# Eight rotary transfers queued behind the next chunk's softmax scaling on GpSimd

## The chip, the cores and the metric

The kernel runs on one core of one Trainium2 chip. The metric is the device time of one execution in microseconds, the median of several runs. The core's engines work side by side, each through its own queue in order: TensorE (PE, matmuls and transposes; its weight loads are listed as PEld), VectorE (DVE), ScalarE (ACT), GpSimd (POOL) and SyncE (SP, which here only issues DMA transfers).

## The reference, cut to what matters

One encoder block over 16 learned meta tokens and 1024 input tokens, width 1024. A combined projection feeds a retention branch (4 heads) and a windowed softmax attention (8 heads in 2 groups, head size 128); both are gated, projected, merged, projected again, normalised and added to the input. The change lies in the attention and its rotary positions:

```python
def _rotary(t, pos):
    ...
    t1, t2 = tf[..., :half], tf[..., half:]
    return jnp.concatenate([t1 * cos - t2 * sin, t2 * cos + t1 * sin], axis=-1)

# attention: each block of 128 queries sees its own and the two neighbouring blocks
# of keys within +-128, 16 meta keys, and a learned sink logit per head
m = jnp.maximum(jnp.max(s, axis=-1, keepdims=True), sink_l)
p = jnp.exp(s - m)
p = p / (jnp.sum(p, axis=-1, keepdims=True) + jnp.exp(sink_l - m))
```

## The kernel before

The program is written in a tile language: the source gives the work and its priority, a scheduler with a model of the engines' times fixes each engine's order, and semaphores are placed by dependence. `tc.issue_after(i)` (and `follow`, which stacks several of them) adds the rule that what is issued inside stands behind instruction `i` in the queue of the same engine. TensorE's order in the attention stage is thus written out by hand: almost everything follows `latest`, the last matmul so far.

All matmuls are done in three products of a high and a low half (`mm3`, lines 76 to 78), so that each operand is first split: a rounded high half on ScalarE (or GpSimd, `pool_hi`, line 89) and the remainder on VectorE (`dve_lo`, line 92).

**The attention's chunks.** There are 32 chunks: four pairs of heads `hp`, each with eight blocks `n` of 128 queries; chunk 8 hp + n. Iteration k of the loop in `attention` does four things in this order on TensorE:

- `stage1` of chunk k + 1: the scores (`ps`), then on VectorE the mask and row minimum (`nm`, line 1423), on ScalarE the exponentials (line 1426), on VectorE the reciprocal of the sum (`den`, line 1430), on GpSimd the scaling of both sides by `den` (line 1439) and two small copies of the meta columns (`pm2`, line 89).
- `stage2` of chunk k: transposes of the scaled weights (`pt`, lines 1455 to 1460), then their split into `pah`/`pal`, `pbh`/`pbl` and `pm`.
- `fill`: a number of projection steps for later chunks, from a list of generators. `FILL` gives the number per chunk: 9, 9, 7, 7, 7, 7, 6, 6 for the first head pair, 7 each for the second, 7, 6, 6, 6, 6, 6, 6, 5 for the third, then 5.
- `stage3` of chunk k - 1: the weights times the values (`po`).

So a chunk's scaling has one `fill` and one `stage3` in which to be done before TensorE needs it.

**The projection steps.** The steps of all `fill`s are numbered through. A block of queries (`aq{hp}_{i}{e}`: head pair, half of the tokens, head of the pair; 512 columns) or of keys (`ak{g}_{i}`: group, quarter of the tokens) takes eight steps, one for each slice of the inputs. At the end of the eighth, `rope_late` turns the block: VectorE multiplies it by sine into `m` and by cosine into `o` (lines 184, 185), and GpSimd issues two transfers (line 187) that add the two halves of `m`, swapped, onto `o`. Key blocks are 256 or 272 columns wide, each transfer of one 64 partitions. GpSimd's queue works in order, so an issue waits there for VectorE's products, and what is behind it waits too.

**The hooks.** The table `BEGUN` says which other work is issued at which step: among it `split_q(hp, e, i)`, which splits a turned block of queries into `aqh`/`aql` (lines 669 and 92), and `keys(g, i)`, which splits a turned block of keys into `kTh`/`kTl` (lines 715 and 92). Both wait for the landing of that block's two transfers. With `FILL` above, step 23 lies in the `fill` of chunk 2, 31 in chunk 3, 47 in chunk 6, 71 in chunk 9, 79 in chunk 11, 119 in chunk 16, 127 in chunk 18 and 151 in chunk 22. Steps 90 and 91 both lie in chunk 12, 136 and 138 in chunk 19, 126 in chunk 17.

Of the kernel before, what the change touches and what calls it, by code (L numbers as in the profile page):

```python
# [10 lines left out]
ALU = mybir.AluOpType  # L11
# [28 lines left out]
def block_kernel(ctx: ExitStack, tc: tile.TileContext, x0, xT, x, meta, w_in, w_rb, w_ab, w_out, post_w,  # L40
                 rope, tab, out):
    nc = tc.nc
# [31 lines left out]
    def mm3(o, ah, al, bh, bl, first, last, free_group=False):  # L74
        kw = {"skip_group_check": True} if free_group else {}
        nc.tensor.matmul(o, ah, bh, start=first, stop=False, **kw)  # L76
        nc.tensor.matmul(o, al, bh, start=False, stop=False, **kw)  # L77
        latest[:] = [nc.tensor.matmul(o, ah, bl, start=False, stop=last, **kw).ins]  # L78
        return latest[0]
# [8 lines left out]
    def pool_hi(o, i):  # L88
        return nc.gpsimd.tensor_scalar(o, i, 1.0, 1.0, op0=ALU.mult, op1=ALU.mult).ins  # L89
# [87 lines left out]
    cr = ra.tile([P, T], F32, name="cr")  # L177
    sr = ra.tile([P, T], F32, name="sr")

    def rope_late(t, a, b, o, nm):  # L180

        n = b - a
        m = ra.tile([P, 512], F32, tag="m", bufs=4, name=f"m_{nm}")
        nc.vector.tensor_tensor(m[:, 0:n], t[:, 0:n], sr[:, a:b], ALU.mult)
        nc.vector.tensor_tensor(o[:, 0:n], t[:, 0:n], cr[:, a:b], ALU.mult)
        for r in (0, 64):
            nc.gpsimd.dma_start(o[64 - r:128 - r, 0:n], m[r:r + 64, 0:n], accum_op=ALU.add)

    def rope_evac(t, a, b, o, nm):
        n = b - a  # L190
# [250 lines left out]
    def gen_qk(h):  # L441
        w = load_w(w_in, U_QK + h)
        q, kt = [], ra.tile([P, 4, 272], F32, tag="kp", bufs=2, name=f"kr{h}")
        qk[h] = (q, kt)
        for i, (a, b) in enumerate(PIECES):
            t = yield from proj(w, P, a, b, f"pk{h}_{i}")
            rope_late(t, a, b, kt[:, i], f"k{h}_{i}")
            yield
        for i, (a, b) in enumerate(HALVES):
            t = yield from proj(w, 0, a, b, f"pq{h}_{i}")  # L450
            o = ra.tile([P, 512], F32, tag="q", bufs=6, name=f"qr{h}_{i}")
            rope_late(t, a, b, o, f"q{h}_{i}")
            q.append(o)
            yield
# [206 lines left out]
    def split_q(hp, e_, i):  # L661

        o = aq[hp][e_, i].rearrange("p (t q) -> p t q", q=64)
        if (hp, i) not in aqs:
            aqs[hp, i] = [aw.tile([P, 1024], R, tag=f"aq{t}", bufs=2, name=f"aq{t}{hp}_{i}") for t in "hl"], set()
            if len(aqs) == 1:
                aw.tile([P, 48], F32, name="space_aq")
        h, l = (t.rearrange("p (t e q) -> p t e q", e=2, q=64)[:, :, e_] for t in aqs[hp, i][0])
        nc.scalar.copy(h, o)
        dve_lo(l, o, h)  # L670
        aqs[hp, i][1].add(e_)
# [18 lines left out]
    def gen_aq(hp, i, es=(0, 1)):  # L690
        if not i:
            if hp not in wq:
                wq[hp] = load_w(w_in, U_AQ + hp)
            aq[hp] = {}
        a, b = HALVES[i]
        for e_ in es:
            t = yield from proj(wq[hp], P * e_, a, b, f"paq{hp}_{i}{e_}")
            o = ra.tile([P, 512], F32, tag="q", bufs=6, name=f"aq{hp}_{i}{e_}")
            rope_late(t, a, b, o, f"aq{hp}_{i}{e_}")
            aq[hp][e_, i] = o  # L700
            yield
# [158 lines left out]
    softmax, last = [], {}  # L860
# [525 lines left out]
    def attention():  # L1386
# [4 lines left out]
        def window(n, x_):  # L1391

            if n == 0:
                return 0, 272, (late_mask if x_ else mask[0][:, 144:416]), [(0, 0), (1, 128)], 256
            start = 272 * ((n - 1) // 2) + 128 * ((n - 1) % 2) + 64 * x_
            wid = (208 if x_ else 272) if n == 7 else 336
            own, moff = (128, 256) if n % 2 else (144, 128)
            blocks = [(n - 1, -64 * x_), (n, own - 64 * x_), (n + 1, 272 - 64 * x_)]
            return start, wid, mask[0][:, 0:wid], blocks[:2 if n == 7 else 3], moff - 64 * x_

        def stage1(hp, n):
            g = hp // 2
            kh, kl = (t.rearrange("p a b -> p (a b)") for t in kT[g])
            i = n // 4
            nm_ = ap.tile([P, 2], F32, tag="nm", bufs=3, name=f"nm{hp}_{n}")
            den = ap.tile([P, 2], F32, tag="den", bufs=3, name=f"den{hp}_{n}")
            pp = weights[n % 2]
            sides = []
            for e_ in range(2):
                if (hp, i) not in aqs or e_ not in aqs[hp, i][1]:  # L1410
                    split_q(hp, e_, i)
            for x_ in range(2):
                start, wid, seen, blocks, moff = window(n, x_)
                a_, b_ = (t[:, P * (2 * (n % 4) + x_):P * (2 * (n % 4) + x_ + 1)] for t in aqs[hp, i][0])
                s = p2(f"ps{hp}_{n}_{x_}")
                mm3(s[:, 0:wid], a_, b_, kh[:, start:start + wid], kl[:, start:start + wid], True, True)
                if n == 0 and hp:
                    raw[x_] = aw.tile([P, 337], F32, tag=f"raw{x_}", bufs=1, name=f"raw{hp}_{x_}")
                r = raw[x_]
                for c in ({0: (272, 336), 7: (208,)} if x_ else {0: (0,)}).get(n, ()):  # L1420
                    nc.vector.tensor_copy(r[:, c:c + 1], nsink[:, hp:hp + 1])
                o, w0 = (0, 64) if x_ else (1, 1)
                nc.vector.tensor_tensor_reduce(r[:, o:o + wid], s[:, 0:wid], seen, -SCALE,  # L1423
                                               nsink[:, hp:hp + 1], ALU.add, ALU.min, nm_[:, x_:x_ + 1])

                last["exp"] = nc.scalar.activation(pp[:, x_, w0 - o:w0 - o + 1 + wid], r[:, 0:1 + wid], AF.Exp,  # L1426
                                                   scale=-1.0, bias=nm_[:, x_:x_ + 1],
                                                   accum_out=den[:, x_:x_ + 1]).ins
                sides.append((wid, w0, blocks, moff))
            last["sum"] = nc.vector.reciprocal(den, den).ins  # L1430
            softmax.append(last["sum"])
            both = ap.tile([P, 2, 2, NM], F32, tag="pm2", bufs=2, name=f"pm2_{hp}_{n}")
            ends = hp == 3 and n > 5
            for x_, (wid, w0, _, _) in enumerate(sides):
                v = pp[:, x_, w0:w0 + wid]
                if ends:
                    softmax.append(nc.scalar.activation(v, v, AF.Copy, scale=den[:, x_:x_ + 1]).ins)
                else:
                    nc.gpsimd.tensor_scalar(v, v, den[:, x_:x_ + 1], 1.0, op0=ALU.mult, op1=ALU.mult)  # L1439
            for x_, (_, w0, _, moff) in enumerate(sides):  # L1440
                w_ = pp[:, x_, w0 + moff:w0 + moff + NM].unsqueeze(1).to_broadcast([P, 2, NM])
                if ends:
                    softmax.append(nc.scalar.copy(both[:, x_], w_).ins)
                else:
                    pool_hi(both[:, x_], w_)
            pt = [lambda o, x_=x_, w0=w0: pp[:, x_, w0 + o:w0 + o + P] for x_, (_, w0, _, _) in enumerate(sides)]
            st1[hp, n] = (pt, [b for _, _, b, _ in sides], both.rearrange("p a b c -> p (a b c)"))

# [62 lines left out]
        with follow(*latest):  # L1511
            stage1(0, 0)
        for k, (hp, n) in enumerate(chunks):
            ends = k >= len(chunks) - 2
# [4 lines left out]
            if k + 1 < len(chunks):  # L1519
                with follow(*latest, *marks("oa", "lo")):  # L1520
                    stage1(*chunks[k + 1])
                if chunks[k + 1] == (1, NB - 1):
                    keys(1, 0)
# [18 lines left out]
            if k in (12, 14, 21):  # L1542
# [11 lines left out]
             61: [(sum_row, 2, 0)], 62: [(sum_row, 2, 1)], 65: [(sum_fetch, 3)], 66: [(split_q, 1, 0, 1)],  # L1554
             68: [(half_w, 'k', 1, 0)], 72: [(half_w, 'k', 1, 1)], 73: [(split_q, 1, 1, 1)], 75: [(sum_row, 3, 0)],
             76: [(sum_row, 3, 1)], 79: [(sum_fetch, 4)], 82: [(split_q, 2, 0, 0)], 88: [(sum_row, 4, 0)],
             89: [(sum_row, 4, 1)], 90: [(split_q, 2, 1, 0)], 92: [(sum_fetch, 5)], 100: [(sum_row, 5, 0)],
             101: [(sum_row, 5, 1)], 102: [(fetch_aq, 3)], 104: [(keys, 1, 1)], 105: [(sum_fetch, 6)],
             110: [(split_q, 2, 0, 1)], 116: [(keys, 1, 2)], 117: [(half_w, 'q', 3, 0)], 121: [(half_w, 'q', 3, 1)],
             122: [(pre_fetch, 9)], 123: [(sum_row, 6, 0)], 124: [(sum_row, 6, 1)], 126: [(split_q, 2, 1, 1)],  # L1560
             127: [(sum_fetch, 7)], 133: [(pre_sum, 9, 0)], 134: [(pre_sum, 9, 1)], 136: [(keys, 1, 3)],
             139: [(pre_sum, 9, 2)], 140: [(pre_parts, 9)], 141: [(pre_fetch, 10)], 145: [(split_q, 3, 0, 0)],
             146: [(sum_row, 7, 0)], 147: [(sum_row, 7, 1)], 150: [(split_q, 3, 1, 0)], 152: [(pre_sum, 10, 0)],
             153: [(pre_sum, 10, 1)], 155: [(pre_sum, 10, 2)], 157: [(pre_parts, 10)], 158: [(pre_fetch, 11)],
# [117 lines left out]
```

## Time and profile before

| | |
|---|---|
| median of 3 runs | 1039.92 us (1038.98 to 1040.74) |
| the profiled execution | 1040.1 us |
| its span, first to last instruction | 1038.3 us |
| TensorE / weight loads busy | 99% / 86% |
| VectorE / ScalarE / GpSimd busy | 80% / 48% / 22% |
| granted TensorE clock | 0.999 |
| the attention stage | about 326 to 545 us of the span |

All places in time are us from the span's start in the profiled execution. A row of the view in order of time gives start, duration, engine, line, operation, tiles and, in brackets, the idle time of the engine before it with what ended that. A matmul counts as busy from its start to its modelled end, and successive matmuls overlap, so a short wait of TensorE shows as a later start and not as idle time. A row of a wait gives the engine and line that waited, who was waited for, the sum in us, the number of times and the longest.

### The profile page before, as it was taken

Reading aid. Unit: us, or ns where it says so; the run is one execution under the profiler, and the core shown is the slowest. Engines: PE = TensorE matmul, PEld = TensorE weight load, DVE = VectorE, ACT = ScalarE, POOL = GpSimd, SP = SyncE. Lnnn points to the kernel's source line nnn. Section 1 sums busy time; section 2 is a strip of 40 time slices with the busy share of each in tenths; the row PEclk is TensorE's granted clock in tenths of the full one; section 3 lists DMA queues with packets and bytes.
Section 4 is the critical chain, followed back from the end, with each engine's and each line's share of the span. In section 5 each row is a group of like instructions: output and inputs, shape, how many; then the busy total and the mean of one; then the engine's idle time right before and its main releaser. Section 6 shows DMA issues by size and latency. Waiting matters only on the chain. (4 is left out here: it accounts for less than half of the span.)

```text
span 1038.3 us, 17311 instructions
## 1 busy us (share of the span) xinstructions
PE 1023.7 (99%) x5883; PEld 898.0 (86%) x5883; DVE 835.8 (80%) x1802; ACT 502.6 (48%) x1129; POOL 228.0 (22%) x368
## 2 busy tenths in 40 slices
PE   9999999999999999999999999999999999999997
PEld 8998999989989888988888888878888788788886
DVE  7886758768875778778769989999899799778665
ACT  5531432423424566665667554455567446334442
POOL 3445244243342333444310000000000000111032
PEclk9999999999999999999999999999999999999999
DMA  9433123243241466675559679899935746789464
GB/s 357 164 87 88 65 47 84 78 88 104 78 93 62 103 182 189 175 188 161 168 176 326 209 260 338 294 330 365 373 102 178 252 153 226 231 231 325 127 122 81
DMA packets 98840, 188.45 MB, mean 181 GB/s; under 512 B 13024, under 2 KB 37632, under 8 KB 98192
## 3 DMA queue, kind: packets, MB, share of 16 engines
q1 hardware_dynamic: 81200, 162.89, 46.6%
q0 software_dynamic: 10176, 14.73, 9.6%
q10 hardware_dynamic: 7376, 9.73, 2.7%
q8 instruction: 46, 0.75, 0.3%
q14 instruction: 42, 0.34, 0.1%
HBM read 124.32 MB, written 57.68 MB: 175 GB/s over the span
## 5 line engine op out<-in xcount | busy, mean ns | idle before, releaser
L1286 POOL DMA_DIRECT2D mx_d<-c1a x4 | 3.6, 890 | 395.8 <-DVE c1a L1277 377.2
L77 PE MATMUL bz<-big,llz 128*128 128x512 f32 x192 | 74.8, 390 | 0.2 <-DVE llz L92 0.2
L78 PE MATMUL bz<-big,lhz 128*128 128x512 f32 x192 | 74.4, 389 | 0.0
L76 PE MATMUL bz<-big,lhz 128*128 128x512 f32 x192 | 74.0, 390 | 0.3 <-ACT lhz L978 0.3
L76 PE MATMUL pv<-wh,big 128*128 128x256 f32 x256 | 72.8, 284 | 0.0
L77 PE MATMUL pv<-wh,big 128*128 128x256 f32 x256 | 72.7, 284 | 0.0
L78 PE MATMUL pv<-wl,big 128*128 128x256 f32 x256 | 72.7, 284 | 0.0
L76 PE MATMUL bz<-T,lhz 128*128 128x512 f32 x176 | 68.1, 390 | 1.1 <-DVE u2z L1068 1.1
L78 PE MATMUL bz<-T,lhz 128*128 128x512 f32 x176 | 68.5, 389 | 0.0
L77 PE MATMUL bz<-T,llz 128*128 128x512 f32 x176 | 68.5, 389 | 0.0
L76 PE MATMUL paq<-big,wh 128*128 128x512 f32 x128 | 51.6, 403 | 0.0
L1426 ACT ACTIVATE p<-raw,nm 128x337 f32<-128x337 f32 (+1 forms) x64 | 35.5, 556 | 32.2 <-DVE nm L1423 30.6
L77 PE MATMUL paq<-big,wl 128*128 128x512 f32 x128 | 50.2, 392 | 0.0
L78 PE MATMUL paq<-big,wh 128*128 128x512 f32 x128 | 50.2, 392 | 0.0
L1439 POOL TENSOR_SCALAR p<-p,den 128x336 f32<-128x336 f32 (+2 forms) x60 | 34.6, 624 | 66.5 <-DVE den L1430 59.1
L76 PEld LDWEIGHTS pv<-wh,big 128*128 128x128 f32 x256 | 48.3, 189 | 0.4
L77 PEld LDWEIGHTS pv<-wh,big 128*128 128x128 f32 x256 | 48.3, 189 | 0.4
L78 PEld LDWEIGHTS pv<-wl,big 128*128 128x128 f32 x256 | 48.2, 188 | 0.3
L92 DVE TENSOR_TENSOR wl<-wr,wh 128x1024 fp32r<-128x1024 f32 x28 | 35.1, 1258 | 10.4 <-POOL wh L89 6.7
L76 PEld LDWEIGHTS bz<-big,lhz 128*128 128x128 f32 x192 | 36.1, 188 | 8.1 <-ACT lhz L978 0.7
L77 PEld LDWEIGHTS bz<-big,llz 128*128 128x128 f32 x192 | 36.0, 188 | 7.9 <-DVE llz L92 0.5
L78 PEld LDWEIGHTS bz<-big,lhz 128*128 128x128 f32 x192 | 36.0, 188 | 7.5
(621 smaller groups left out, 3594.6 us busy)
## 6 DMA issues: line engine op xcount, KB each, us to landing
wrz<-in_w_in_dram SPq DMA_DIRECT2D x32, 512.0 KB, 6.1
wr<-in_w_in_dram SPq DMA_DIRECT2D x29, 512.0 KB, 4.1
we<-in_w_in_dram SPq DMA_DIRECT2D x16, 512.0 KB, 4.3
tg<-tg_d SPq DMA_DIRECT2D x32, 256.0 KB, 5.1
e<-e ACTq DMA_DIRECT2D x20, 256.0 KB, 2.7
e<-e SPq DMA_DIRECT2D x20, 256.0 KB, 5.3
xn<-in_x_dram SPq DMA_DIRECT2D x8, 512.0 KB, 9.5
oTr_d<-ost SPq DMA_DIRECT2D x16, 256.0 KB, 2.1
```

The costliest lines, as they stand in the source:

```text
L76: nc.tensor.matmul(o, ah, bh, start=first, stop=False, **kw)
L77: nc.tensor.matmul(o, al, bh, start=False, stop=False, **kw)
L78: latest[:] = [nc.tensor.matmul(o, ah, bl, start=False, stop=last, **kw).ins]
L92: return nc.vector.tensor_tensor(o, i, hi.bitcast(F32), ALU.subtract).ins
L1286: nc.gpsimd.dma_start(d, to, accum_op=ALU.add)
L1426: last["exp"] = nc.scalar.activation(pp[:, x_, w0 - o:w0 - o + 1 + wid], r[:, 0:1 + wid], AF.Exp, scale=-1.0, bias=nm_[:, x_:x_ + 1], accu ...
L1439: nc.gpsimd.tensor_scalar(v, v, den[:, x_:x_ + 1], 1.0, op0=ALU.mult, op1=ALU.mult)
```

## The change

The names of eight blocks are listed in `BEHIND`. For these, `rope_late` keeps the two transfers back in a list, `held`. At the end of `stage1` of the next chunk that is emitted, after its scalings and meta copies, the transfers are issued with the rule that they stand behind the last of those copies in GpSimd's queue. Since iteration k + 1 emits `stage1` of chunk k + 2, a block turned in the `fill` of chunk k has its transfers behind the scaling of chunk k + 2. Two hooks move: `split_q(2, 1, 0)`, which reads `aq2_01`, from step 90 to 91, and `keys(1, 3)`, which reads `ak1_3`, from 136 to 138. What is computed does not change.

```diff
+    held = []
+    BEHIND = "aq1_00", "aq1_01", "aq1_10", "aq2_00", "aq2_01", "aq2_11", "ak1_3", "aq3_10"
+
     def rope_late(t, a, b, o, nm):
...
         nc.vector.tensor_tensor(m[:, 0:n], t[:, 0:n], sr[:, a:b], ALU.mult)
         nc.vector.tensor_tensor(o[:, 0:n], t[:, 0:n], cr[:, a:b], ALU.mult)
-        for r in (0, 64):
-            nc.gpsimd.dma_start(o[64 - r:128 - r, 0:n], m[r:r + 64, 0:n], accum_op=ALU.add)
+
+        def rotate():
+            for r in (0, 64):
+                nc.gpsimd.dma_start(o[64 - r:128 - r, 0:n], m[r:r + 64, 0:n], accum_op=ALU.add)
+        if nm in BEHIND:
+            held.append(rotate)
+        else:
+            rotate()
...
                 if ends:
                     softmax.append(nc.scalar.copy(both[:, x_], w_).ins)
                 else:
-                    pool_hi(both[:, x_], w_)
+                    last["scaled"] = pool_hi(both[:, x_], w_)
+            if not ends:
+                with tc.issue_after(last["scaled"]):
+                    while held:
+                        held.pop(0)()
...
-             89: [(sum_row, 4, 1)], 90: [(split_q, 2, 1, 0)], 92: [(sum_fetch, 5)], 100: [(sum_row, 5, 0)],
+             89: [(sum_row, 4, 1)], 91: [(split_q, 2, 1, 0)], 92: [(sum_fetch, 5)], 100: [(sum_row, 5, 0)],
...
-             127: [(sum_fetch, 7)], 133: [(pre_sum, 9, 0)], 134: [(pre_sum, 9, 1)], 136: [(keys, 1, 3)],
+             127: [(sum_fetch, 7)], 133: [(pre_sum, 9, 0)], 134: [(pre_sum, 9, 1)], 138: [(keys, 1, 3)],
```

## Prediction, made before the result

> **What bounds the kernel now.** I read the page first, then busy time by stretch, then TensorE's waits in the attention stage, and last GpSimd, VectorE and TensorE in order of time around the eight moved transfers.
>
> ```profile
> PE 1023.7 (99%) x5883; PEld 898.0 (86%) x5883; DVE 835.8 (80%) x1802; ACT 502.6 (48%) x1129; POOL 228.0 (22%) x368
> 326.00:545.00 219.00, 216.65 (x1315) 192.36 (x1314) 163.70 (x432) 132.57 (x358) 74.21 (x156) 1.00 0.59 164
> PE pt L1455 <- POOL p L1439: 0.7, 2, 0.5
> PE pt L1459 <- DVE pbl L92: 0.4, 1, 0.4
> PE pt L1455 <- DVE pal L92: 0.4, 1, 0.4
> PE pt L1460 <- POOL pm L89: 0.2, 1, 0.2
> ```
>
> TensorE is busy 99% of 1038.3 us; all other engines matter only where they make it wait. The second line is the attention stage (stretch, length, then busy time of TensorE, weight loads, VectorE, ScalarE, GpSimd): TensorE is idle there for 219.00 - 216.65 = 2.35 us, at a granted clock of 1.00. The change touches nothing outside this stage, so it can win two or three microseconds; what it can lose has no such ceiling, since TensorE's order is written out by hand and a late operand stops it.
>
> The idle figures understate the stalls, because a matmul still counts as busy while the next one waits. I therefore take the time from a chunk's first transpose to the projection matmul after it, once where nothing waits (a chunk with six data transposes, then one with four) and then at the stalls:
>
> ```profile
> 372.01 0.60 PE L1455 MATMUL pt<-ident,p 128*128 128x128 f32 x4
> 372.69 0.48 PE L76 MATMUL pe<-big,weh 128*128 128x512 f32 x1
> 439.76 0.60 PE L1455 MATMUL pt<-ident,p 128*128 128x128 f32 x4
> 440.23 0.36 PE L76 MATMUL pak<-big,wh 128*128 128x256 f32 x1
> ...
> 386.27 0.66 PE L1455 MATMUL pt<-ident,p 128*128 128x128 f32 x4
> 386.95 0.48 PE L76 MATMUL paq<-big,wh 128*128 128x512 f32 x1
> 421.16 0.31 PE L1455 MATMUL pt<-ident,p 128*128 128x128 f32 x1
> 422.18 0.37 PE L76 MATMUL pak<-big,wh 128*128 128x272 f32 x1
> 464.84 0.31 PE L1455 MATMUL pt<-ident,p 128*128 128x128 f32 x1
> 466.01 0.48 PE L76 MATMUL paq<-big,wh 128*128 128x512 f32 x1
> 492.92 0.33 PE L1455 MATMUL pt<-ident,p 128*128 128x128 f32 x1
> 494.57 0.48 PE L76 MATMUL paq<-big,wh 128*128 128x512 f32 x1
> ```
>
> Undisturbed it is 0.68 us, or 0.47 us with four. The chunk at 386 took 0.68 (0.21 over), at 421 1.02 (0.34 over), at 464 1.17 (0.49 over), at 492 1.65 (1.18 over). Together 2.22 us.
>
> **Part 1: the scalings that come earlier.** In these four chunks GpSimd issued a rotation (two transfers) just before the scaling that the transposes need. Of the last of them, and of one where the scaling lost nothing (first number the start, second the duration):
>
> ```profile
> 490.37 1.68 POOL L187 DMA_DIRECT2D aq<-m_aq  x2 [7.22 <-ACT pah L1465]
> 491.50 2.19 POOL L1439 TENSOR_SCALAR p<-p,den 128x272 f32<-128x272 f32 x2
> 489.76 0.16 DVE L1430 RECIPROCAL den<-den 128x2 f32<-128x2 f32 x1
> ...
> 359.46 0.17 DVE L1430 RECIPROCAL den<-den 128x2 f32<-128x2 f32 x1 [0.87 <-ACT p L1426]
> 359.80 1.08 POOL L1439 TENSOR_SCALAR p<-p,den 128x336 f32<-128x336 f32 x2 [0.20 <-DVE den L1430]
> ```
>
> At 490 the reciprocal was there at 489.92, yet the scalings ended at 491.50 + 2.19 = 493.69, also stretched by running into the descriptor writing. Undisturbed, a scaling starts 0.18 us after its reciprocal (359.63 to 359.80) and the pair takes 1.08: it would end at 491.2, before the transposes at 492.92. So 1.18 us goes whole. The other three have the same shape, so I credit their full 0.21, 0.34 and 0.49. At the remaining four (the rotations at 357.9, 365.6, 408.0 and 454.6) I credit nothing: the row at 359.80 shows the scaling there waited for its reciprocal, and the transfers were out of the way by then. The gain in front of the doubtful place below is 0.21 + 0.34 = 0.55 us; behind it 1.18; the 0.49 lies right before it.
>
> **Part 2: the transfers that come later.** A rotation made in the projection steps of chunk k is now issued behind the scaling of chunk k+2. For the two whose rows stand below it is 3.6 and 6.5 us. For most, nobody needs that time: `aq1_00`, `aq1_10` and `aq2_00` land before ScalarE's splits reach them, and `aq1_01`, `aq2_01` and `aq3_10` are read by score matmuls four or five chunks later, so only ScalarE, busy 132.57 of 219 us, can be held for a moment. I cost these at nothing; the cover is ScalarE's slack, and if it is gone, rival two shows the price. One is different, `ak1_3`, the last piece of keys:
>
> ```profile
> 462.50 1.68 POOL L187 DMA_DIRECT2D akr<-m_ak  x2 [4.54 <-DVE akr L185]
> 467.23 1.08 POOL L1439 TENSOR_SCALAR p<-p,den 128x336 f32<-128x336 f32 x2 [1.45 <-DVE den L1430]
> 468.27 0.40 POOL L89 TENSOR_SCALAR pm<-p 128x32 f32<-128x32 f32 x2
> L187 POOL DMA_DIRECT2D akr<-m_ak x2: 843/980/1117, 462.5 to 463.1; - x2
> DMA to landing us min/median/max: 3.4/3.7/3.9
> 468.03 0.41 ACT L715 CAST kTh<-akr 128x256 fp32r<-128x256 f32 x1
> 470.90 0.41 DVE L92 TENSOR_TENSOR kTl<-akr,kTh 128x256 fp32r<-128x256 f32 x1
> 471.39 0.32 PE L76 MATMUL ps<-kTh,aqh 128*128 128x336 f32 x1
> ...
> DMA to landing us min/median/max: 2.3/2.5/2.7
> DMA to landing us min/median/max: 7.7/7.7/7.7
> ```
>
> It is made in step 127, in the projections of chunk 18, so its transfers go from ahead of scaling 19 (462.50) to behind scaling 20 (467.23, with its copies until 468.67). The score matmuls of chunk 21 (third head pair, n = 5, columns 544 to 880 of the keys) start at 471.39 and read this piece, which begins at column 816. In before its low half was finished only at 471.31. Worked out: 468.67, plus 0.28 from end to issue (the row of 359.80 gives 0.2 after a transfer; I take a little more), is 468.95, less the 0.55 already won is 468.40. The second transfer follows 0.6 later (the pair started at 462.5 and 463.1): 469.0. It landed up to 3.9 us after its issue in before (the first landing row is that of this pair): 472.9. ScalarE's copy of 0.41 makes it 473.3, and the low half 0.41 later is needed one matmul pair (0.32) on, another 0.1. So the score matmuls end their wait about 2.0 us later than in before, and the 0.49 won at 464 vanishes in that wait. The step's move from 136 to 138 changes nothing here: it puts the copy where it can't stand in front of ScalarE's earlier work, but the landing is later than either place.
>
> The two other landing rows, for earlier key pieces, are the bounds: with 2.7 us the wait ends 0.8 us later than in before instead of 2.0, with 7.7 us it is 5.8.
>
> **The sum.** +2.0 at chunk 21, -1.18 at the stall of 492, which stays removable since it is relative to its own chunk: +0.8 us. The profiled execution took 1040.1 us, so 1040.9; it stood 0.2 above the median of 1039.92, so I forecast a median of **1040.7 us**, "no change" within the 0.2% (2.1 us) that a measurement of this kernel can about tell. With the landing bounds it is 1039.5 to 1044.5.
>
> **Rivals.**
>
> *One, the transfer lands quickly.* The pair of 2.3 to 2.7 us speaks for it, this pair's own 3.4 to 3.9 against it. Then 0.8 - 1.18 = -0.4 us, 1039.5. The Trainium skill (DMA: Bandwidth & Descriptors, "Anatomy of one DMA — SWDGE (gpsimd) path") fits such a transfer as about 2.0 us plus its bytes over 436e3, so an estimated 2.15 us for 64 KB. By that rule the wait would end 0.55 us sooner still and the sum would be an estimated -0.9 us. The trace agrees with it only at its shortest landing of 2.3. The chance is 0.14.
>
> *Two, ScalarE stands in front of its softmax work (slower).* `aq2_11` moves from 454.63 to behind scaling 18, and its split in step 126 has not been moved.
>
> ```profile
> 452.17 0.41 ACT L715 CAST kTh<-akr 128x256 fp32r<-128x256 f32 x1 [1.76 <-DMA akr<-m_ak]
> 454.63 1.69 POOL L187 DMA_DIRECT2D aq<-m_aq  x2 [4.37 <-DVE aq L185]
> 457.56 0.39 POOL L89 TENSOR_SCALAR pm<-p 128x32 f32<-128x32 f32 x2
> DMA to landing us min/median/max: 3.1/3.3/3.4
> 459.50 0.61 ACT L669 CAST aqh<-aq 128x512 fp32r<-128x512 f32 x1
> 460.27 0.58 ACT L1426 ACTIVATE p<-raw,nm 128x337 f32<-128x337 f32 x1
> ```
>
> Issued at 457.95 + 0.28, the second one 0.6 later, it lands 3.4 us on, at 462.2, while the split stands at 459.50, ahead of chunk 19's exponentials. If that order is kept, ScalarE waits 2.7 us, and behind it queue the copy of the output, two exponentials and the casts of chunk 18, then VectorE's low halves, then the scores of chunk 20 and scaling 20, behind which `ak1_3` itself waits. All of it moves by 2.7 us: +0.8 + 2.7 = +3.5 us, 1043.4. It decides if the split is still placed before the exponentials at 460.27. For it: the transposes' waits on `pal` and `pbl` in the list above (0.8 us of idle, near 457) came after just such a wait, 1.76 us for a transfer at 452.17. Against it: the program is scheduled with modelled transfer times, which should move the split back, and `aq2_11` is not read before chunk 20's scores. Chance 0.23.
>
> *Three, no late key (faster).* If the new order lets scaling 20 run early enough, or the scheduler's other moves hide the wait, all 2.22 us are won: 1037.7. For it: GpSimd is only 74 of 219 us busy, so nothing of its own holds the transfers back. Against it: scaling 20 needs chunk 20's own scores, which TensorE gives at its own pace, so no reordering gains the 2 us fully. Chance 0.17; it may reach a little lower if the 0.8 us on `pal` and `pbl` go as well.
>
> *Four, a landing like 7.7 us* (seen once among these pieces): +5.8 - 1.18 = +4.6, 1044.5. Chance 0.10.
>
> **How the numbers follow.** Forecast 0.36, rivals 0.14, 0.23, 0.17 and 0.10. Faster by over 0.2% means below 1037.8: rival three, and a little of one, 0.18. Slower means above 1042.0: rivals two and four and a little of the forecast, 0.34. Within: 0.48. The range of eight in ten reaches from rival three's 1037.7, with 0.2 us of room, to just over rival two, 1037.5 to 1043.9; it leaves out rival four and the depth of three. The likeliest case alone, with landings between 2.7 and about 4.8 us, is 1039.5 to 1041.6.
>
> **What would show it.** Right: the transposes at about 421, 464 and 492 follow each other without a wait for `p`; the scalings take 1.1 us again; a new wait of some 2 us stands at the score matmuls of chunk 21 (near 471), for `kTh` or `kTl`, with a transfer issued after 468 behind it. Wrong: no wait at those scores (rival three); a ScalarE wait of over 2 us for `aq` near 459 with its exponentials behind it (rival two). If the time falls by more than 2.3 us, part 1 missed something the scalings held up.

## The result: 0.36% slower

| | before | after |
|---|---|---|
| median of 6 runs, same chip | 1040.01 us (1038.98 to 1040.74) | 1044.07 us (1042.48 to 1045.37) |
| the profiled execution | 1040.1 us | 1044.08 us |
| its span | 1038.3 us | 1042.3 us |

The ratio is 1.0036, with a 95% interval of 1.0025 to 1.0047: some 4 us slower. The forecast was 1040.7 us, "no change" at 0.48, with 0.34 on slower. The line of busy times on the page of after, then the attention stage in the view by stretches (length, busy time of TensorE, weight loads, VectorE, ScalarE, GpSimd, then granted clock, DMA share, GB/s), then TensorE's waits in that stage:

```profile
PE 1024.7 (98%) x5883; PEld 898.3 (86%) x5883; DVE 835.3 (80%) x1802; ACT 502.5 (48%) x1129; POOL 227.0 (22%) x368
```
```profile
326.00:545.00 219.00, 213.83 (x1299) 190.00 (x1298) 163.33 (x431) 131.48 (x356) 72.66 (x156) 1.00 0.57 159
```
```profile
PE ps L76 <- ACT kTh L724: 1.6, 1, 1.6
PE ps L76 <- ACT aqh L678: 1.2, 1, 1.2
PE ps L77 <- DVE aql L92: 1.2, 3, 0.6
PE pt L1473 <- POOL pm L89: 1.1, 1, 1.1
```

(Line numbers have moved: the transfers are now line 192, the scaling 1448, the exponentials 1435, the splits of queries and keys 678 and 724, the transposes 1468 to 1473.) The work is the same, and the granted clock is 1.00. TensorE's idle time in the stage went from 2.35 to 219.00 - 213.83 = 5.17 us. The waits of before on `p`, `pal` and `pbl` are gone from the list. In their place stand longer ones: score matmuls for `kTh` and for `aqh`/`aql` (of the three on `aql`, 0.5 us at the start of the stage is in before too, and 0.6 belongs to chunk 28), and a transpose for `pm`.

As idle time understates a stall, I matched TensorE's matmuls of the two executions one by one and took, at each chunk's last transposes, how far after is behind before. It starts the stage 0.14 us behind. Where this lag moves by more than 0.1 us:

| chunk (its place in before) | change of the lag, us | what TensorE meets |
|---|---|---|
| 7 (386), 12 (421) | -0.19, -0.34 | the scaling is in time, as forecast |
| 16 (446) | +1.26 | transposes wait for `pm` |
| 18 (459) | -1.11 | the wait on `pal`, `pbl` of before is covered |
| 19 (466) | +1.56 | scores of chunk 20 wait for `aqh`, `aql` (+1.93), less what chunk 19's own transposes win |
| 20 (473) | +1.83 | scores of chunk 21 wait for `kTh` |
| 23 (494) | -1.17 | the scaling is in time, as forecast |
| 27 (519) | +1.34 | scores of chunk 28 wait for `aql` |
| after the attention | +0.71 | |

With the start that is +4.0 us, the difference of the two spans. The last row may be no more than the spread of single executions: in the profiles of the other kernels below, the same part of the program is between 0.4 us shorter and 1.4 us longer than in before.

**The gains came.** Transposes and the projection matmul after them, in after's view in order of time, to be read against the rows in the prediction:

```profile
421.09 0.60 PE L1468 MATMUL pt<-ident,p 128*128 128x128 f32 x4
...
421.77 0.37 PE L76 MATMUL pak<-big,wh 128*128 128x272 f32 x1
...
496.02 0.60 PE L1468 MATMUL pt<-ident,p 128*128 128x128 f32 x4
...
496.48 0.48 PE L76 MATMUL paq<-big,wh 128*128 128x512 f32 x1
```

From first transpose to projection 0.68 us at 421 (1.02 before) and 0.46 at 496 (1.65 before): undisturbed.

**The late blocks.** GpSimd, ScalarE and TensorE of after in order of time:

```profile
457.93 1.69 POOL L192 DMA_DIRECT2D aq<-m_aq  x2 [0.18 <-issue]
460.82 0.58 ACT L1435 ACTIVATE p<-raw,nm 128x337 f32<-128x337 f32 x1 [0.15 <-DVE nm L1432]
463.61 0.28 PE L1503 MATMUL po<-pm,vm 128*128 128x256 f32 x1
464.46 0.62 ACT L678 CAST aqh<-aq 128x512 fp32r<-128x512 f32 x1 [2.50 <-DMA aq<-m_aq]
465.13 0.57 PE L76 MATMUL ps<-kTh,aqh 128*128 128x336 f32 x2 [1.25 <-ACT aqh L678]
...
469.12 1.08 POOL L1448 TENSOR_SCALAR p<-p,den 128x336 f32<-128x336 f32 x2 [5.47 <-DVE den L1439]
470.75 1.68 POOL L192 DMA_DIRECT2D akr<-m_ak  x2 [0.18 <-issue]
472.63 0.28 PE L1503 MATMUL po<-pm,vm 128*128 128x256 f32 x1
474.01 0.41 ACT L724 CAST kTh<-akr 128x256 fp32r<-128x256 f32 x1 [0.70 <-DMA akr<-m_ak]
474.47 0.42 PE L76 MATMUL ps<-kTh,aqh 128*128 128x336 f32 x1 [1.57 <-ACT kTh L724]
```

And the two pairs of transfers in the view of their tiles, with the shortest, median and longest time from issue to landing:

```profile
L192 POOL DMA_DIRECT2D aq<-m_aq x2: 841/987/1133, 457.9 to 458.5; - x2
...
DMA to landing us min/median/max: 4.2/5.1/5.9
```
```profile
L192 POOL DMA_DIRECT2D akr<-m_ak x2: 841/982/1123, 470.7 to 471.3; - x2
...
DMA to landing us min/median/max: 2.3/2.5/2.6
```

`aq2_11` was issued in its place (457.93; forecast 457.95 + 0.28) but took up to 5.9 us, so ScalarE stood still for 2.50 us and the scores of chunk 20 began only at 465.13. `ak1_3` landed in 2.3 to 2.6 us, but its scaling had itself moved: 469.12 and not 467.23, since chunk 20's scores were late. So the scores of chunk 21 waited too.

### The profile page after: what moved, and what is told of

It reads as the page before. It is cut to its first block, busy times and chain, and to the rows that moved or that the text cites. A ratio compares the mean times of both kernels' runs of the same rounds, so it can differ in the third digit from the quotient of the medians.

```text
span 1042.3 us, 17311 instructions
## 1 busy us (share of the span) xinstructions
PE 1024.7 (98%) x5883; PEld 898.3 (86%) x5883; DVE 835.3 (80%) x1802; ACT 502.5 (48%) x1129; POOL 227.0 (22%) x368
## 5 line engine op out<-in xcount | busy, mean ns | idle before, releaser
L1448 POOL TENSOR_SCALAR p<-p,den 128x336 f32<-128x336 f32 (+2 forms) x60 | 31.9, 552 | 119.7 <-DVE den L1439 114.9
```

## Experiments

**Theory A**: the price is two blocks, `aq2_11` and `ak1_3`, which land too late for the next scores and are each paid in full. **Rival B**: the two waits cover each other (a later chunk gives `ak1_3` more time), so that taking one away wins nothing. **Rival C**: the new order of GpSimd's and ScalarE's queues as a whole costs, whichever block is late. Each ratio is to runs of the kernel before on the same chip.

**One of the two set free.** `ak1_3`, or `aq2_11`, is taken from the list and issued at once, as in before:

```diff
-    BEHIND = ..., "aq2_01", "aq2_11", "ak1_3", "aq3_10"
+    BEHIND = ..., "aq2_01", "aq2_11", "aq3_10"
```


> The change without ak1_3 in the list of held blocks; keys(1,3) stays at step 138. Theory A (the loss is two late landings, each paid by TensorE in full): the wait for kTh at the scores of chunk 21 (1.6 us of idle, 1.8 us of delay) goes, the one for aqh at chunk 20 stays: 1042.2 us, +2.2 on before. Rival B (the two waits cover each other, the time stands until the later of them): under 0.5 us better than the change, about 1043.6. Rival C (no single transfer, the scheduler's new order as a whole): anything from 1041 to 1045, and the waits turn up in other places.

```diff
+    BEHIND = ..., "aq2_01", "ak1_3", "aq3_10"
```


> The change without aq2_11 in the list. Theory A: the wait for aqh and aql at the scores of chunk 20 (1.9 us of delay) goes, that for kTh at chunk 21 stays at about 1.8: 1042.1 us. Rival B: ak1_3 then lands no earlier against TensorE, so chunk 21 waits about 3.5 us and the time is about 1043.6. Rival C: 1041 to 1045.

**Both set free:**

```diff
+    BEHIND = ..., "aq2_01", "aq3_10"
```


> The change without ak1_3 and aq2_11: six blocks held, both hooks moved. Theory A: 1044.0 less 1.8 and 1.9, 1040.3 us, about the time before; what is left over against the full gain of 2.2 us are the new wait for pm at chunk 15 (1.3 us) and for aql at chunk 28 (1.1 us), where no late landing is seen. Rival B: the same 1040.3, since both are gone. Rival C: 1041 to 1045.

Measured: without `ak1_3` 1042.55 us, ratio 1.0017 (1.0008 to 1.0026); without `aq2_11` 1041.98, 1.0012 (1.0003 to 1.0020); without both 1040.06, 0.9992 (0.9984 to 1.0001). From 1.0036 the first is worth 0.19%, the second 0.24%, both 0.44%: they add up within their intervals, so B falls and A holds for the change as it is made. By the table, 1.56 + 1.83 = 3.4 us of the 4.6 us that go with both are the two waits themselves; most of the rest is the wait at chunk 28, which falls from +1.34 to +0.26. TensorE's waits, first without `ak1_3`, then without `aq2_11`, then without both:

```profile
PE ps L76 <- ACT aqh L678: 1.8, 1, 1.8
```
```profile
PE ps L76 <- ACT kTh L724: 1.7, 1, 1.7
...
PE pt L1473 <- POOL pm L89: 0.7, 1, 0.7
```
```profile
PE ps L77 <- DVE aql L92: 0.5, 1, 0.5
PE pt L1472 <- DVE pbl L92: 0.4, 1, 0.4
```

Each wait goes with its own block. With both free the other two of after, for `pm` at chunk 16 and for `aql` at chunk 28, have left the list too (the 0.5 us on `aql` is the one at the start of the stage). The one at chunk 28 stays as long as either block is held (+1.49 without `ak1_3`, +1.25 without `aq2_11`).

**One of the two alone.** From the other side: only that block is held, the other seven go at once, with the hooks moved as in the change; and the hooks moved with nothing held.

```diff
+    BEHIND = ("ak1_3",)
```


> ak1_3 alone is held; both hooks moved. Theory A (each late landing costs by itself): the scores of chunk 21 wait for kTh, 1.8 us of delay, the stall at chunk 19's transposes (0.5) goes, the other gains stay out: ratio 1.0013, about +1.3 us. Rival C (the order as a whole): no set time, 0 to +4, and no such wait in the trace.

```diff
+    BEHIND = ("aq2_11",)
```


> aq2_11 alone is held; both hooks moved. Theory A: ScalarE waits for its landing some 2.5 us, the scores of chunk 20 wait for aqh and aql, 1.6 to 1.9 us of delay, with none of the gains but what chunk 18 got: ratio 1.0016, about +1.7 us. If the landing is as short as before's (3.4 us after issue) the wait is under 0.5 us. Rival C: 0 to +4, no such wait.

```diff
+    BEHIND = ()
```


> The list of held blocks is empty, the two hooks stay at 91 and 138: the second half of the change alone. Theory A: neither split is read soon, so the ratio is 1.000 within 0.001, and the wait for pm at chunk 16, which the change has, is not there if it comes from aq2_01's late transfers; if it comes from the moved hooks it is there and costs 0.3 to 1.3 us.

Measured: `ak1_3` alone 1043.28 us, 1.0025 (1.0016 to 1.0034); `aq2_11` alone 1041.44, 1.0010 (1.0001 to 1.0019); the hooks alone 1040.89, 1.0001 (0.9992 to 1.0010). The hooks cost nothing that can be measured. `ak1_3` costs by itself about twice the 0.13% that A gave it, and that lies outside the interval: in the matching its wait is +2.84 us, against 0.47 us won at chunk 19, and a lower clock after the wait adds 1.19 us (last section). `aq2_11` alone costs less than half of the 0.24% that it costs in the change; the interval holds A's 1.0016 too, so the trace has to decide. Its landing rows, alone and (second) in the kernel without `ak1_3`:

```profile
L192 POOL DMA_DIRECT2D aq<-m_aq x2: 795/934/1074, 458.1 to 458.6; - x2
...
DMA to landing us min/median/max: 2.9/3.2/3.6
```
```profile
L192 POOL DMA_DIRECT2D aq<-m_aq x2: 841/986/1131, 457.6 to 458.2; - x2
...
DMA to landing us min/median/max: 4.2/5.3/6.4
```

Alone it was issued half a microsecond later and landed 2.4 us earlier (458.6 + 3.6 = 462.2 against 458.2 + 6.4 = 464.6); neither ScalarE nor the scores waited. At the chunks' last transposes its TensorE was never more than 0.2 us from before's through the whole stage (what it lost came behind the stage, +1.2 us). So place in the queue and landing time together decide.

**The two together, the six others as before:**

```diff
+    BEHIND = "aq2_11", "ak1_3"
```


> Only aq2_11 and ak1_3 are held back, the other six blocks as before; hooks moved as in the change. Alone they gave 1.0010 and 1.0025. Theory A, with prices that belong to each block: the sum, 1.0035, some 1043.7; if aq2_11 lands in under 4 us as it did alone, its part is nothing in the attention stage and the ratio is that of ak1_3 alone, 1.0025. Rival C (aq2_11 is late only in the company of the other six): its transfer lands in under 4 us, ScalarE has no wait near 462, the ratio is 1.0025 or below. If it takes 5 us or more here too, the six others have nothing to do with it, and a wait of 1.2 to 1.8 us stands at the scores of chunk 20. A separate question is the granted clock: where TensorE stands still for 2.0 us or more at chunk 20 or 21, the clock should fall to 0.5 some 2 to 4 us later and stay there for about 3.4 us; with waits up to 1.9 us it should stay at 1.0.

1043.32 us, 1.0022 (1.0013 to 1.0032): about the price of `ak1_3` alone, and A's sum of 1.0035 lies outside the interval. `aq2_11` was issued at 457.96 and landed in 4.0 to 4.4 us; ScalarE waited 0.77 us, TensorE not at all. That is between the two expectations for this block and nearer to C's: it stops TensorE only in the company of the six. In the three profiles where the six are held with it (the change, without `ak1_3`, and the next experiment) it took 5.9, 6.4 and 5.9 us, where they are not 4.4 and 3.6, and the large weight load issued behind it (`we`, near 459.5) was slower too, 5.6, 6.1 and 5.6 us against 4.5 and 4.2. None of the six is itself in flight at 458, but the traces' records of DMA packets show another difference. In the three, the load's first packets come 1.2 us after the first ones of `aq2_11`, when 148 to 150 of the pair's 256 KB had started; in the two, 1.8 us after, when 238 KB had. Where `aq2_11` is issued in its old place or one scaling earlier, the load comes 4.6 us after, behind the whole pair, and the landing takes at most 3.6 us. So with the six the load runs into the second half of these transfers. No run moves the load by itself: that it makes the landing late is argued from this order, not shown.

**The wait for `pm` at chunk 16.** In after the transfers of `ak1_2`, which is not in the list, went between the two copies of the meta columns:

```profile
443.69 0.96 POOL L1448 TENSOR_SCALAR p<-p,den 128x272 f32<-128x272 f32 x2 [2.86 <-DVE den L1439]
444.62 0.21 POOL L89 TENSOR_SCALAR pm<-p 128x32 f32<-128x32 f32 x1
444.88 1.69 POOL L192 DMA_DIRECT2D akr<-m_ak  x2
445.99 0.83 POOL L89 TENSOR_SCALAR pm<-p 128x32 f32<-128x32 f32 x1
```

The second copy started 1.2 us after the first one's end and took 0.83 us, not 0.21; a transpose waited for it. To put that right, `ak1_2` is issued behind both copies:

```diff
         else:
-            rotate()
+            with follow(*(marks("scaled") if nm == "ak1_2" else [])):
+                rotate()
```


> The change, and the transfers of ak1_2, which is not in its list, are put behind the meta copies of chunk 16's scaling, where the scheduler of the change put them between the two copies. If the wait for pm at chunk 16 (1.3 us of delay in the change) comes from that place in the queue: the wait goes and the ratio falls from 1.0036 to about 1.0025. If it comes from the late exponentials in front of it (ScalarE waited 2.6 us for a load): the delay is still there in most part, and the ratio stays near 1.0035.

1044.3 us, 1.0032 (1.0019 to 1.0044): the interval holds both expected ratios, so the trace decides. The wait for `pm` is gone, as the first of the two expected, and yet nothing is won. The lag came two chunks later instead, at chunk 18 (+0.93), where the transposes waited 1.3 us for `pal`:

```profile
PE pt L1469 <- DVE pal L92: 1.3, 1, 1.3
```

The transfers, some 6.4 us from issue to landing in both kernels, were issued at 446.06 and not at 444.88, so ScalarE got the keys 1.4 us later (453.32 against 451.96) and `pal` behind them was late. Early, they are in the way of `pm`; late, they are late for chunk 18, where before had its stall on `pal` and `pbl` from the same block. In after the two places nearly cancel (+1.26 and -1.11): of the 4 us only 0.15 is there.

**The same idea, one scaling earlier.** Two kernels put transfers behind the scaling that was emitted last, that of chunk k + 1 for a block turned in the projections of chunk k, and not behind that of k + 2. The first, made from before, does so for every block and leaves the hooks; the second is the change with its eight blocks and its hooks:

```diff
-        for r in (0, 64):
-            nc.gpsimd.dma_start(...)
+        with follow(*marks("scaled")):
+            for r in (0, 64):
+                nc.gpsimd.dma_start(...)
...
-                    pool_hi(both[:, x_], w_)
+                    last["scaled"] = pool_hi(both[:, x_], w_)
```


> Not the change, but before with every rotation made in the projections of chunk k put behind the scaling of chunk k+1, the last that has been issued by then, in place of k+2; hooks as in before. Only rotations that would have gone in between that scaling and its TensorE use are held, ak1_3 by about 1.8 us in place of 8, aq2_11 not at all. Theory A: the 2.2 us of stalls behind held-up scalings go and no landing is late: 1037.8 us. Rival C: the scheduler's order moves again, 1039 to 1042. If ak1_3 is late even so: a wait for kTh at chunk 21 and about 1039.

```diff
         if nm in BEHIND:
-            held.append(rotate)
+            with follow(*marks("scaled")):
+                rotate()
```


> The change's eight blocks and its two moved hooks, but each pair of transfers stands behind the scaling that was emitted last before it (chunk k+1) instead of the one after (k+2). Theory A (the price of the change is that two blocks land too late for the scores that read them): aq2_11 and ak1_3 are issued one chunk, some 4 to 5 us, earlier, no score matmul waits over 0.6 us, the four gains at the transposes stay: ratio 0.998 to 0.9995, some 1038.5 to 1039.5. Rival C (the new order as a whole costs, whatever block is late): the copies and transfers around chunks 16 and 28 still wait and the ratio stays at 1.000 or above; then the earlier gain with every block behind its next scaling came from the blocks that are not in this list.

The first took 1038.79 us, ratio 0.9984 (0.9975 to 0.9992), the second 1038.78 us, 0.9986 (0.9977 to 0.9995). Both are faster than both kernels of this case: by the ratios some 1.5 us under before and 5 us under after. Of the second, the stage by stretches, TensorE's waits in it (all of them), and the landing rows of `aq2_11` and `ak1_3`:

```profile
326.00:545.00 219.00, 217.41 (x1329) 194.07 (x1328) 163.99 (x434) 133.21 (x360) 73.00 (x156) 1.00 0.59 164
```
```profile
PE pt L1469 <- DVE pal L92: 0.6, 1, 0.6
PE ps L77 <- DVE aql L92: 0.5, 1, 0.5
PE pt L1473 <- DVE pbl L92: 0.4, 1, 0.4
PE bz L77 <- DVE llz L92: 0.2, 1, 0.2
```
```profile
L192 POOL DMA_DIRECT2D aq<-m_aq x2: 843/982/1122, 455.6 to 456.1; - x2
...
DMA to landing us min/median/max: 2.7/3.0/3.2
```
```profile
L192 POOL DMA_DIRECT2D akr<-m_ak x2: 846/982/1117, 465.5 to 466.1; - x2
...
DMA to landing us min/median/max: 3.7/3.9/4.1
```

TensorE's idle time in the stage is 219.00 - 217.41 = 1.59 us, against 2.35 in before and 5.17 in after. `ak1_3` is issued 5.2 us earlier than in after and lands at 466.1 + 4.1 = 470.2 at the latest, though its transfers took longer than in after; the scores no longer wait for a key. In the same matching against before this kernel gains 0.19 us at chunk 7, 0.33 at 12, 0.48 at 19 and 1.18 at 23: together 2.18 us, where the prediction had 2.22 for them. Smaller losses at chunks 3, 16 and 18 (0.18, 0.26, 0.19) leave 1.5. C therefore falls for the change as a whole: the same eight blocks in a new order, with the same hooks, are a gain as soon as the two doubtful ones land in time. A stands, with the limit that `aq2_11` stops TensorE only in the company of the others.

## Where the prediction was right and where wrong

**Right.** Part 1: the four stalls are removable and worth what the transposes show (0.19, 0.34 and 1.17 us in after against 0.21, 0.34 and 1.18; the fourth, 0.49 at chunk 19, is 0.48 in the kernel with the eight blocks one scaling earlier). `ak1_3` makes the scores of chunk 21 wait, forecast 2.0 us, 1.83 in the matching, and the 0.49 of chunk 19 vanishes in a wait. Rival four's landing of 7.7 us did not come for it. Rival one's quick landing did occur for `ak1_3`: 2.6 us, where the Trainium skill's fit (DMA: Bandwidth & Descriptors, "Anatomy of one DMA — SWDGE (gpsimd) path") gave an estimated 2.15, and yet there was no gain, because the scaling that it stood behind was 1.9 us late. The forecast had the right wait there with a wrong split: 2.0 came from a landing of 3.9 us behind a scaling at 467.23. That 2.0 and 1.83 agree is luck: a later scaling and a shorter landing nearly cancelled. That the mechanism is right shows where `ak1_3` is held alone: with its scaling in time TensorE is 2.84 - 0.47 = 2.4 us late there.

**Wrong: the sum puts `aq2_11` at nothing.** Part 2 gives its reasons for six blocks ("I cost these at nothing") and a price for `ak1_3`; `aq2_11` stands in rival two alone, and the forecast has neither a term nor a reason for it. For the six the zero roughly holds: without the two blocks the ratio is 0.9992. For `aq2_11` rival two has an issue at 457.95 + 0.28 and the landing of before, 3.4 us; the issue was right to 0.3 us and the landing was 5.9. The term is +1.93 us at the scores of chunk 20 (+1.56 behind chunk 19's transposes), and it pushed chunk 20's scaling, and with it `ak1_3`, back as well. It was rival two's block, and its chain (ScalarE, scores of chunk 20, scaling 20, `ak1_3`) is the one that ran; but its deciding condition, a split placed ahead of chunk 19's exponentials, was not met. The split stands behind them, ahead of `pm` and `pbh` of chunk 18, and was late all the same. By rival two the end was 1043.4 us. The result is a median of 1044.07, or 1039.92 x 1.0036 = 1043.7 on the prediction's own base, at the upper end of the range of 1037.5 to 1043.9. That the two are so close is partly luck: rival two had 2.7 us for `aq2_11`, where 1.93 was measured, and it had nothing for the next two terms. What I should have done is what I did for `ak1_3`: set the bounds of 2.7 and 7.7 us beside this landing too. From 458.5 with 5.9 us the block arrives at 464.4, and its scores were due at 463.7.

**Not foreseen:** the wait at chunk 28 (+1.34) and what came behind the attention (+0.71), together half of the 4.0 us. Chunk 28's scores wait there for the low half `aql`, which VectorE finishes at 520.64 at the end of a row of splits. VectorE had waited 1.58 us for a load of `we` at 508 (0.74 in before). The lateness is there from that load on: the addition behind it starts 3.86 us later than in before (508.36 and 504.50), the split of `aql` 3.85 us later (519.96 and 516.11), while TensorE is 1.93 us late. The load was issued 3.0 us later (503.2 and 500.2) and took 5.1 us instead of 4.2, just after the four transfers of two query blocks issued in one go. Where only two transfers stand there, as in before and with the eight blocks one scaling earlier, the load takes 4.2 us and nothing is lost; with four it takes 4.5 us without both blocks (+0.26), 5.0 without `aq2_11` (+1.25) and 5.3 without `ak1_3` (+1.49). So four transfers alone don't give the wait. It was not tried by itself: the load is a suspicion and the cause stays open, as does that of the 0.71. The wait for `pm` was not foreseen either, but it cost nothing in the sum.

## What to carry to other kernels

To take a queue's slow step out of an urgent one's way, put it just behind the step that it delays and no further: the same eight transfers cost 0.36% behind the scaling of chunk k + 2 and won 0.14% behind that of k + 1. For each thing moved, work out its landing with the longest duration that the profile shows for such a transfer, not its own last one, and set that against its first reader. An operand that is late for the busiest engine is paid in full, and everything that is queued behind that engine's result moves with it.

## What the hardware showed

**The clock can fall after a wait of 2 us.** In the kernel that holds `ak1_3` alone, TensorE started a matmul at 471.03 and the next at 473.45 (2.15 us idle), and 1.2 us later the granted clock fell (the view in order of time, then by stretches, where the clock stands behind GpSimd's busy time):

```profile
473.45 0.42 PE L76 MATMUL ps<-kTh,aqh 128*128 128x336 f32 x1 [2.15 <-ACT kTh L724]
...
476.63 0.63 PE L78 MATMUL paq<-big,wh 128*128 128x512 f32 x1
477.06 0.63 PE L76 MATMUL paq<-big,wh 128*128 128x512 f32 x1
```
```profile
474.00:475.00 1.00, 1.00 (x9) 0.99 (x8) 0.47 (x1) 0.00 (x0) 0.00 (x0) 0.84 0.87 281
475.00:476.00 1.00, 1.00 (x6) 0.96 (x5) 0.59 (x4) 0.80 (x3) 0.00 (x0) 0.50 1.14 244
476.00:477.00 1.00, 1.00 (x3) 0.77 (x3) 0.23 (x2) 1.00 (x4) 0.20 (x1) 0.50 0.54 92
477.00:478.00 1.00, 1.00 (x4) 0.74 (x3) 0.89 (x2) 0.68 (x3) 1.00 (x3) 0.50 0.02 2
478.00:479.00 1.00, 1.00 (x6) 0.83 (x5) 0.97 (x4) 0.00 (x0) 0.24 (x2) 0.95 0.00 0
```

For about 3.4 us (0.32 + 3 + 0.1 from these slices) the clock was 0.5 and 512-column matmuls came 0.43 us apart, not 0.23, which added 1.19 us to the lag. That was a gap of 2.42 us from start to start. The kernel without `ak1_3` shows the same after one of 2.06 us. With gaps of 1.52 to 2.01 us (after, twice; the two blocks together; the kernel without `aq2_11`) the clock stayed at 1.00. The Trainium skill (TensorE: Matmul & The Clock Gate, "Part 1: The HAM clock gate (the "warmup" mystery)") says that the clock halves after an idle window of about 3.4 us and comes back after one that is busy. The length of the slow stretch agrees; here gaps of 2.06 and 2.42 us were enough, so a wait shorter than the stated window can cost half its length again. The timed runs show it too. A stretch of 3.4 us at half clock lowers a run's mean granted clock by 1.7 / 1041 = 0.0016. That mean is 0.998 or 0.999 in 80 of 81 runs of before and in all 9 with both blocks, but 0.996 or 0.997 in 8 of the 11 runs with `ak1_3` alone. These 8 took 1043.4 us on average, the other three 1042.1: 1.2 us apart, as in the profile. The same low mean stands in 4 of 12 runs without `ak1_3`, in 5 of 11 without `aq2_11` (its one profile has a gap of 2.01 us and no fall) and in 1 of 6 of the change. A part of these kernels' prices is therefore the clock, above all with `ak1_3` alone: about 1.0017 by its three other runs.

**Equal transfers land very unequally.** The pair of `aq2_11`, issued between 457.6 and 458.1 in four kernels, took at most 3.6, 4.4, 5.9 and 6.4 us. The two long ones had a load's packets 1.2 us behind their own first ones, the two short ones 1.8 us.
